# A hybrid gMLP / RG-LRU layer in FP32 on one core: a merge-gate tile joins each turn of the recurrent loop, merge gates wait in DRAM, and the loop's GpSimd work moves to VectorE and ScalarE

## The chip, the cores and the metric

The kernel runs on one core of a Trainium2 chip. Its engines are TensorE (PE in the rows, its weight loads PEld), VectorE (DVE), ScalarE (ACT), GpSimd (POOL) and SyncE (SP), which here only issues DMAs. Each engine carries out its own instructions strictly in program order and waits, at the head of its list, for whatever an instruction needs from another engine. The metric is the device time of one launch in microseconds.

## The reference

The kernel computes one layer of a diffusion backbone for 128 context tokens and 1024 latent tokens (1152 in all) of width 1024, all in FP32:

```python
h = rmsnorm(x, g_pre_mix) * (1 + sc1) + sh1
u, v, xr, gr, ga, gb = split(h @ w_in)             # six blocks of 1024 columns
y_g = sgu(gelu(u), gelu(v), ...)                   # spatial gating in chunks of 128 tokens
xc = depthwise_conv(xr, width 4)
r, ig = sigmoid(block_diag(xc) + b)                # per direction, 16 heads of 64 channels
a = exp(-8 * r * softplus(-lam)); bx = sqrt(1 - a*a) * ig * xc
h_rnn = scan_forward(a, bx) + scan_backward(a, bx) # h[t] = a[t] h[t-1] + bx[t]
y_r = h_rnn * gelu(gr)
merged = sigmoid(ga) * (y_g @ w_br_g) + sigmoid(gb) * (y_r @ w_br_r)
x = x + g1 * rmsnorm(merged @ w_out)
x = x + g2 * rmsnorm(relu(h2 @ w_ff1)**2 @ w_ff2)
```

The six modulation vectors (sh1, sc1, g1, sh2, sc2, g2) are products of a conditioning vector with `w_ada`; the last four are built on VectorE in the middle of the kernel.

## The kernel before

**Column tiles.** Channels lie on the partitions and tokens along the row. Most of the work is a series of "column tiles": 128 output channels for all 1152 tokens, in three chunks of 384 tokens, contracted over 8 blocks of 128 channels. To keep FP32 accuracy each operand is split into a high and a low part, and a product is three passes (high x high, high x low of the data, low of the weights x high), so a tile is 8 x 3 x 3 = 72 matmuls of 128x384. A tile named `xr`, `gr`, `ga`, `gb`, `u` takes its columns from `w_in`; `br` and `bg` are the two branch projections.

**Weights.** The list `stream` (lines 88 to 97) holds the tiles in the order in which TensorE takes them. `w_load` fetches a tile's raw weights by a DMA on SP, `w_hi` makes the high part `wh` (a cast, L120 on ScalarE or L122 on GpSimd), `w_lo` the low part `wl` (a subtraction on VectorE, L129), and `w_convert` does both. `w_next`, at the start of a tile, converts what is not yet converted and issues the loads of the next two.

**Banks.** A tile fills one of two groups of three PSUM banks (`P3`), in turn; the group is free again when its eviction has read it.

**The recurrent loop** (lines 564 to 625, nine turns). Turn j computes the tiles `xr(j+1)` and `gr(j+1)`, and between their matmuls, after the 12th and 30th of xr and the 30th and 54th of gr, the four gate steps `g` (L442, six matmuls each), each followed by two tanh on ScalarE (L448). Beside that, VectorE does the convolution of the next tile (L421, L425), the decay (L478, L479), the input terms, two scans (L498) and the low parts. GpSimd does the high parts of the next two weight tiles (L122), the gate weights' cast (L400), and `finish` (L499): the sum of the two scans and its product with the GELU gate (L504, L506), whose result it stores to DRAM (`d_yr`, L508). The GELU of gr(j+1) is taken at the start of the next turn. The last two turns run gb0 to gb3 in place of xr and gr, and gb4 follows.

**The merge gates.** gb0 to gb4 are held in SBUF as `tb`. The loop over the `br` tiles multiplies each by its gate (L705) and stores it to DRAM (`d_mr`); gb5 to gb7 stand between br0 to br3, and after each of these eleven tiles VectorE takes one step of the later modulations (`ada_steps`: four passes over two blocks of `w_ada`, L675 or L677); a finished modulation is summed over partitions by an all-reduce on GpSimd (L660). Then come ga0 and ga1 with eight loads of v weights (`wv_load`, four after each), the v matmuls (`pv`), ga2 to ga7, the u tiles and the bg tiles, which read the `ta` gates from SBUF.

All temporaries share one pool of 48 SBUF slots.

Of the kernel before, what the change touches and what calls it, by code (L numbers as in the profile page):

```python
# [8 lines left out]
F32 = mybir.dt.float32  # L9
# [5 lines left out]
P = 128  # L15
# [10 lines left out]
# columns of the packed per-channel vectors, each block [channel % 128, channel // 128]  # L26
# [6 lines left out]
def tile_layer(ctx: ExitStack, tc: tile.TileContext, x, vec, rows, bsp, w_spT, ident_in, w_ada1, w_ada, w_in, w_gate,  # L33
# [28 lines left out]
    d_yr = [tc.dram_tile([P, NT], F32, name=f"d_yr{j}") for j in range(KT - 1)]  # L62
    d_x1 = [tc.dram_tile([P, D], F32, name=f"d_xa{t}") for t in range(NTT)]
    d_mod = [[tc.dram_tile([1, D], F32, name=f"d_mod{m}{v}") for v in range(2)] for m in range(4)]

    # ---------------------------------------------------------------- constants
# [7 lines left out]
    # silu of the two conditioning vectors, interleaved [k, (sample, prompt)]  # L74
# [11 lines left out]
    # ---------------------------------------------------------------- weights, one 128-column tile at a time  # L86
    w_in_cols = {"u": 0, "xr": 16, "gr": 24, "ga": 32, "gb": 40}
    stream = []
    for j in range(KT):
        stream += [("xr", j), ("gr", j)]  # L90
    stream += [("gb", 0), ("gb", 1), ("gb", 2), ("gb", 3), ("gb", 4)]
    for j in range(KT):
        stream += [("br", j)] + ([("gb", j + 5)] if j + 5 < KT else [])
    stream += [("ga", j) for j in range(KT)]
# [40 lines left out]
    def w_next(kind, j, ahead=True, load=True):  # L135
        """the split tile of this position; the next one is split meanwhile, the one after it loaded"""
# [17 lines left out]
    def colmm(ps, W, X, cs=range(NC3), ks=range(KT), between=None, at=()):  # L154
        """ps[:, c, :CW] = (W_hi + W_lo).T @ (X_hi + X_lo), without lo * lo; a step of `between` at some points"""
# [11 lines left out]
    # ---------------------------------------------------------------- first norm, first modulation (sh1, sc1)  # L167
# [4 lines left out]
    # the two vectors, hi in columns 0 and 1 and lo in columns 2 and 3 of a full stationary tile  # L172
# [50 lines left out]
    # softplus(-lam) = max(-lam, 0) + log1p(exp(-|lam|)); log1p(e) = 2 atanh(e / (2 + e))  # L223
# [32 lines left out]
    def warm_up(n):  # L256
        """matmuls for their time alone, which keep the tensor engine at its full clock over a wait"""
        for i in range(n):
            pe.matmul(pm1[0], sils[:, 0, :], sils[:, :4, :].rearrange("p k n -> p (k n)"), start=True, stop=True)
# [69 lines left out]
    with tc.tile_pool(name="pa", bufs=2, space=PSUM, reuse_waits="tile") as pa:  # L329
# [34 lines left out]
        def k_both(k):  # L364
            """the passes with X_lo last"""
# [29 lines left out]
        # ------------------------------------------------------------ recurrent branch  # L395
# [168 lines left out]
        for j in range(KT + 1):  # L564
            more = j + 1 < KT
            kx, kg = ((("xr", j + 1), ("gr", j + 1)) if more else (("gb", 2 * (j + 1 - KT)), ("gb", 2 * (j + 1 - KT) + 1)))
            if pgr and j < KT:
                gg[j] = gelu(pgr)
# [601 lines left out]
```

## Time and profile before

| | us |
|---|---|
| three runs: lowest, median, highest | 1852.48, 1853.08, 1853.35 |
| profiled execution, its span | 1852.7 |
| TensorE busy in it | 1798.5 (97%) |
| VectorE, ScalarE, GpSimd busy | 988.3, 621.6, 208.1 |

The profiled execution gives its span alone and no other time; it stands 0.4 us below the median of the runs. Times in the rows are microseconds from the start of the span; `x3` is the number of instructions that a row holds, `[5.06 <-issue]` is the idle time of that engine just before the row and what ended it, where "issue" means that the profile shows no releaser. In the views by stretch, PEclk is the TensorE clock that was granted, 1.00 being 2.4 GHz and 0.50 being 1.2 GHz. Shapes are partitions x elements.

### The profile page before, as it was taken

The page shows a single profiled execution, that of the slowest core. Times are in us where ns is not written, and L with a number is a line of the kernel's source. Part 1 is how long each engine was busy: PE and PEld are TensorE (multiplying, and loading weights), DVE is VectorE, ACT ScalarE, POOL GpSimd, SP SyncE. Part 2 cuts the span into 40 slices and gives each one's busy share as a digit, 9 for nine tenths or more (in the row PEclk, how much of TensorE's full clock was granted, in tenths as well). Part 3 has the DMA queues.
Part 4 walks back from the last instruction along what each step waited for, and adds up shares of the span by engine and source line. Part 5 has one row for each costly group of instructions (what it writes and reads, how often), then busy time and mean ns, then how long its engine had stood idle before and what let it go on. Part 6 is the DMA issues. An engine that isn't in the chain of part 4 may idle for free.

```text
span 1852.7 us, 22285 instructions
## 1 busy us (share of the span) xinstructions
PE 1798.5 (97%) x9504; PEld 1679.8 (91%) x9504; DVE 988.3 (53%) x1013; ACT 621.6 (34%) x857; POOL 208.1 (11%) x159
## 2 busy tenths in 40 slices
PE   7899889899999999999999999999999999999998
PEld 5799889799998899999988899999999999999996
DVE  6859999985662163225453432444444444444447
ACT  7378766731112221223246643111111111111112
POOL 4203343311320031000001100000000000000001
PEclk9999999899999999999999999999999999999999
DMA  8101111243471031103252401111111111011134
GB/s 333 46 29 46 55 53 55 88 157 133 155 248 41 12 114 46 35 23 121 84 160 91 164 30 46 46 35 46 46 44 37 46 46 38 32 46 46 46 137 159
DMA packets 47506, 148.84 MB, mean 80 GB/s; under 512 B 8984, under 2 KB 9256, under 8 KB 47408
## 3 DMA queue, kind: packets, MB, share of 16 engines
q1 hardware_dynamic: 46400, 143.31, 22.6%
q0 software_dynamic: 1008, 4.13, 0.6%
q8 instruction: 74, 1.21, 0.3%
q14 instruction: 24, 0.20, 0.0%
HBM read 129.09 MB, written 18.33 MB: 80 GB/s over the span
## 4 chain that ended last, share of the span: by engine, by line
PE 78%; DVE 2%; DMA 0%; POOL 0%; issue 0%; DVEq 0%; POOLq 0%; ACT 0%; ACTq 0%
PE pf L152 21%; PE p L1090 7%; PE p L1091 7%; PE p L1089 7%; PE u L152 5%; PE br L152 5%; PE ga L152 5%; PE bg L152 5%; PE gb L152 2%; PE po L934 2%; PE po L935 2%; PE po L933 2%; PE pv L748 2%; PE pv L746 2%; PE pv L747 2%; PE s L784 1%
## 5 line engine op out<-in xcount | busy, mean ns | idle before, releaser
L1074 DVE TENSOR_TENSOR acc<-p,acc 128x512 f32<-128x512 f32 x252 | 169.2, 689 | 113.3 <-PE p L1091 113.2
L1090 PE MATMUL p<-w2l,fh 128*128 128x512 f32 x576 | 224.7, 390 | 0.4 <-DVE w2l L1008 0.4
L1091 PE MATMUL p<-w2h,fl 128*128 128x512 f32 x576 | 224.7, 390 | 0.0
L1089 PE MATMUL p<-w2h,fh 128*128 128x512 f32 x576 | 224.3, 389 | 0.0
L120 ACT ACTIVATE wh<-wr 128x1024 fp32r<-128x1024 f32 x70 | 73.4, 1053 | 330.2 <-PE p L1090 236.8
L152 PE MATMUL pf<-h2l,wh 128*128 128x384 f32 x768 | 178.6, 335 | 0.0
L152 PE MATMUL pf<-h2h,wh 128*128 128x384 f32 x768 | 178.5, 335 | 0.0
L152 PE MATMUL pf<-h2h,wl 128*128 128x384 f32 x768 | 178.2, 334 | 0.0
L1000 DVE TENSOR_TENSOR f<-f 128x1152 f32<-128x1152 f32 x32 | 43.5, 1358 | 252.2 <-ACT f L999 252.2
L152 PEld LDWEIGHTS pf<-h2h,wh 128*128 128x128 f32 x768 | 137.3, 188 | 1.1
L999 ACT ACTIVATE f<-pf 128x384 f32<-128x384 f32 x96 | 40.4, 492 | 291.1 <-PE pf L152 291.1
L152 PEld LDWEIGHTS pf<-h2l,wh 128*128 128x128 f32 x768 | 137.4, 188 | 0.0
L152 PEld LDWEIGHTS pf<-h2h,wl 128*128 128x128 f32 x768 | 137.2, 188 | 0.0
L1090 PEld LDWEIGHTS p<-w2l,fh 128*128 128x128 f32 x576 | 108.2, 188 | 22.9 <-DVE w2l L1008 0.8
L1091 PEld LDWEIGHTS p<-w2h,fl 128*128 128x128 f32 x576 | 108.2, 188 | 22.5
L1089 PEld LDWEIGHTS p<-w2h,fh 128*128 128x128 f32 x576 | 108.2, 188 | 22.1
L129 DVE TENSOR_TENSOR wl<-wr,wh 128x1024 fp32r<-128x1024 f32 x86 | 105.3, 1228 | 40.5 <-ACT wh L120 38.3
L448 ACT ACTIVATE th<-g,hbg 64x1152 f32<-64x1152 f32 x64 | 77.9, 1217 | 49.1 <-PE g L442 40.5
L83 POOL TENSOR_SCALAR ssf<-ssf 128x1 f32<-128x1 f32 x9 | 1.7, 191 | 778.4 <-ACT jk L1021 778.3
L660 POOL PARTITION_ALL_REDUCE adr<-ada x8 | 55.8, 6981 | 241.1 <-PE pv L748 102.7
L677 DVE SCALAR_TENSOR_TENSOR ada<-wa,sil,ada 128x1024 f32<-128x1024 f32 x56 | 72.6, 1356 | 3.0 <-DMA wa<-in_w_ada 3.0
L55 DVE TENSOR_TENSOR fl<-f,fh 128x1152 fp32r<-128x1152 f32 x32 | 43.5, 1358 | 39.5 <-ACT fh L54 39.5
(215 smaller groups left out, 3533.0 us busy)
## 6 DMA issues: line engine op xcount, KB each, us to landing
wa<-in_w_ada SPq DMA_DIRECT2D x48, 512.0 KB, 6.6
wr<-in_w_in SPq DMA_DIRECT2D x40, 512.0 KB, 3.5
wr<-in_w_ff SPq DMA_DIRECT2D x32, 512.0 KB, 3.8
w2r<-in_w_ff SPq DMA_DIRECT2D x32, 512.0 KB, 3.5
x<-in_x SPq DMA_DIRECT2D x9, 512.0 KB, 6.7
d_mr<-mr SPq DMA_DIRECT2D x8, 576.0 KB, 3.2
mrl<-d_mr SPq DMA_DIRECT2D x8, 576.0 KB, 3.8
xe<-in_x SPq DMA_DIRECT2D x9, 512.0 KB, 4.8
```

The lines of the kernel that those rows point to most:

```text
L55: (eng or dve).tensor_tensor(lo, src, f32(hi), op=ALU.subtract)
L120: act.activation(hi, raw, AF.Copy)
L129: (eng or dve).tensor_tensor(lo, wopen.pop(i), f32(hi), op=ALU.subtract)
L152: pe.matmul(ps(c), w[:, k * P:(k + 1) * P], X[k][v](c), start=k == 0 and p == 0, stop=k == KT - 1 and p == 2)
L448: act.activation(chunks(th[2 * d + (g ^ h)][o, :]), ps[q, :, :CW], AF.Tanh, scale=0.5, bias=hbg[q, col:col + 1])
L660: pool.partition_all_reduce(o, t, P, ReduceOp.add)
L677: dve.scalar_tensor_tensor(a[v], raw, sc, a[v], op0=ALU.mult, op1=ALU.add)
L1000: dve.tensor_tensor(f, f, f, op=ALU.mult)
L1074: dve.tensor_tensor(a[:, s], ps[t, h], a[:, s], op=ALU.add)
L1089: pe.matmul(ps, fh, wh, start=start, stop=False)
L1090: pe.matmul(ps, fh, wl, start=False, stop=False)
L1091: pe.matmul(ps, fl, wh, start=False, stop=stop)
```

## The change

Turn j of the loop now runs three column tiles, `xr(j+1)`, `gr(j+1)` and `gb(j)`; turn 7 runs gb7 and ga0, turn 8 ga1 and ga2, and ga3 follows the loop. Then stand all eight br tiles in a row, ga4, the eight v-weight loads, the v matmuls, and ga5 to ga7. All sixteen merge gates go to DRAM after their tanh (`d_tb`, `d_ta`, 576 KB each) and are read again one tile ahead of their use (`tbl`, `tal`). In the loop the casts `w_hi` are ScalarE's, `finish` is VectorE's and its store SP's; GpSimd keeps the gate weights' cast (now L401), one copy of two state columns and the all-reduces. The GELU of gr(j+1) stands right behind its tile. The modulation steps take one place per br tile and a second one after br0, br2, br4 and br6; one follows ga4, three lie in the second half of the v matmuls and three beside ga5 to ga7.

```diff
     d_yr = [tc.dram_tile([P, NT], F32, name=f"d_yr{j}") for j in range(KT - 1)]
+    d_ta = [tc.dram_tile([P, NT], F32, name=f"d_ta{j}") for j in range(KT)]
+    d_tb = [tc.dram_tile([P, NT], F32, name=f"d_tb{j}") for j in range(KT)]
...
     for j in range(KT):
-        stream += [("xr", j), ("gr", j)]
-    stream += [("gb", 0), ("gb", 1), ("gb", 2), ("gb", 3), ("gb", 4)]
-    for j in range(KT):
-        stream += [("br", j)] + ([("gb", j + 5)] if j + 5 < KT else [])
-    stream += [("ga", j) for j in range(KT)]
+        stream += [("xr", j), ("gr", j)] + ([("gb", j - 1)] if j else [])
+    stream += [("gb", KT - 1)] + [("ga", j) for j in range(4)]
+    stream += [("br", j) for j in range(KT)]
+    stream += [("ga", j) for j in range(4, KT)]
...
-        def finish(j, th, eng):
+        def finish(j, th):
             h = th[1]
-            eng.tensor_tensor(h, h, th[3], op=ALU.add)
+            dve.tensor_tensor(h, h, th[3], op=ALU.add)
             y = U("yr")
-            eng.tensor_tensor(y, h, gg.pop(j), op=ALU.mult)
+            dve.tensor_tensor(y, h, gg.pop(j), op=ALU.mult)
             if j + 1 < KT:
-                pool.dma_start(d_yr[j], y)
+                sp.dma_start(d_yr[j], y)
...
-        def gb_tanh(ps):
-            t = U("tb")
+        def gate_tanh(ps, name):
+            t = U(name)
             act.activation(chunks(t), ps[:, :, :CW], AF.Tanh, scale=0.5)
             return t
+        def gb_tanh(j, ps):
+            sp.dma_start(d_tb[j], gate_tanh(ps, "tb"))
+        def ga_tanh(j, ps):
+            sp.dma_start(d_ta[j], gate_tanh(ps, "ta"))
...
         pool.memset(warm, 0.0)
-        gg, xcs, tb = {}, {}, {}
+        gg, xcs = {}, {}
...
             more = j + 1 < KT
-            kx, kg = ((("xr", j + 1), ("gr", j + 1)) if more else (("gb", 2 * (j + 1 - KT)), ("gb", 2 * (j + 1 - KT) + 1)))
-            if pgr and j < KT:
-                gg[j] = gelu(pgr)
+            kx, kg = (("xr", j + 1), ("gr", j + 1)) if more else (("gb", j), ("ga", 0)) if j < KT else (("ga", 1), ("ga", 2))
...
                 xcn = conv(j + 1, xr)
+                del xr
                 nxt = xcn, [U("xs", F32R), U("xs", F32R)]
             else:
-                tb[kx[1]] = gb_tanh(px)
+                if j < KT:
+                    gb_tanh(j, px)
+                else:
+                    ga_tanh(1, px)
...
             pgr = col_matmul(*kg, between=steps, at=(30, 54))
-            i = wpos[0]
-            w_hi(i, pool)
-            w_lo(i)
-            w_hi(i + 1, pool)
             if more:
-                raw, gw = gate_hi(j + 1)
+                gg[j + 1] = gelu(pgr)
+                w_convert(wpos[0])
+            else:
+                ga_tanh(kg[1], pgr)
+            del pgr
...
                 del tpp
-            w_lo(i + 1)
+            if more:
+                raw, gw = gate_hi(j + 1)
+                pgb = col_matmul("gb", j)
+                gb_tanh(j, pgb)
+                del pgb
+            i = wpos[0]
+            w_hi(i)
+            w_lo(i)
+            w_hi(i + 1)
...
                 head_lo(*nxt)
+            w_lo(i + 1)
             if prev:
                 scan(j - 1, 1, xcp, thp, ms[1])
-                late = j - 1, thp, pool if j < KT else dve
+                late = j - 1, thp
                 del xcp, thp, ms
             if j == KT - 1:
                 yr_load(range(3))
-                tb[1] = gb_tanh(pgr)
...
         yr_load(range(3, KT - 1))
-        tb[3] = gb_tanh(pgr)
         finish(*late)
-        del xc, prev, pgr, xr, gw, xcn, steps, late, tps
+        del xc, prev, gw, xcn, steps, late, tps
         yr_split(range(3, KT - 1))
-        tb[4] = gb_tanh(col_matmul("gb", 4))
+        ga_tanh(3, col_matmul("ga", 3))
...
         Y = [(acc(h), acc(l)) for h, l in yrs]
+        tbl = {}
+        def tb_load(j):
+            if j < KT:
+                tbl[j] = U("tbl")
+                sp.dma_start(tbl[j], d_tb[j])
+        def ada_step():
+            ada_row()
+            next(ada, None)
+        tb_load(0)
         for j in range(KT):
             W = w_next("br", j)
+            tb_load(j + 1)
             ps = P3("br")
             colmm(pc(ps), W, Y)
             mr = U("mr")
-            dve.scalar_tensor_tensor(chunks(mr), chunks(tb.pop(j)), 1.0, ps[:, :, :CW], op0=ALU.add, op1=ALU.mult)
+            dve.scalar_tensor_tensor(chunks(mr), chunks(tbl.pop(j)), 1.0, ps[:, :, :CW], op0=ALU.add, op1=ALU.mult)
             sp.dma_start(d_mr[j], mr)
-            ada_row()
-            next(ada)
-            if j + 5 < KT:
-                tb[j + 5] = gb_tanh(col_matmul("gb", j + 5, ahead=True))
-                ada_row()
-                next(ada)
+            ada_step()
+            if j % 2 == 0:
+                ada_step()
         del Y, yrs, mr
-        tha = []
...
             colmm(pc(ps), W, X)
-            t = U("ta")
-            act.activation(chunks(t), ps[:, :, :CW], AF.Tanh, scale=0.5)
-            tha.append(t)
+            ga_tanh(j, ps)
-        ga_matmul(0)
-        ada_row()
-        next(ada)
-        for k in range(4):
+        ga_matmul(4)
+        for k in range(KT):
             wv_load(0, k)
-        ga_matmul(1)
-        for k in range(4, KT):
-            wv_load(0, k)
-        ada_row()
-        next(ada)
+        ada_step()
...
                     wv_load(1, t)
+                if h == 1 and t in (1, 4, 7):
+                    ada_step()
...
                     act.activation(vt[h * 4 + g][:, t, :], ps[:, g * P:(g + 1) * P], AF.Gelu_apprx_tanh)
+            for k in range(KT):
+                del wv[h, k]
...
                 dve.reduce_sum(ssv[:, g, :], jk, axis=mybir.AxisListType.X)
-        wv.clear()
...
         sp.dma_start(bspt, bsp.to_broadcast([P, KT * P]).rearrange("p (g q) -> p g q", g=KT))
-        for j in range(2, KT):
+        for j in range(5, KT):
             ga_matmul(j)
-            ada_row()
-            next(ada, None)
-            if j == 2:
+            ada_step()
+            if j == 5:
                 dve.reduce_sum(ssum, ssv.rearrange("p g t -> p t g"), axis=mybir.AxisListType.X)
                 rsqrt_mean(rv[:, :NTT], ssum, 1e-6)
-            for g in ((0, 1, 2) if j == 2 else (j,)):
+            for g in range(3 * (j - 5), min(3 * (j - 4), KT)):
...
         mg = [None] * 3
-        mrl = {0: None}
+        mrl, tal = {}, {}
...
             sp.dma_start(mrl[j], d_mr[j])
+            tal[j] = U("tal")
+            sp.dma_start(tal[j], d_ta[j])
...
             colmm(pc(ps), W, Y)
-            t = tha[j]
-            tha[j] = None
+            t = tal.pop(j)
```

Three places show how the instructions move; a name's number is that of its buffer.

On ScalarE, around the end of a gr tile in a turn of the loop, before (`th` are the gates' tanh, `xs` the high part of the convolved tile, `gg` the GELU of gr):

```order
L448 ACTIVATE th_2144<-g_2179,hbg 64x1152
L448 ACTIVATE th_2143<-g_2179,hbg 64x1152
L457 ACTIVATE xs_2104<-xc_2095 64x1152
L514 ACTIVATE gg_2242<-gr_2112 128x1152
L448 ACTIVATE th_2259<-g_2261,hbg 64x1152
L448 ACTIVATE th_2260<-g_2261,hbg 64x1152
L448 ACTIVATE th_2260<-g_2288,hbg 64x1152
L448 ACTIVATE th_2259<-g_2288,hbg 64x1152
```

and in the changed kernel (`wh` are high parts of weights, `tb` a merge gate's tanh):

```order
L449 ACTIVATE th_2570<-g_2605,hbg 64x1152
L449 ACTIVATE th_2569<-g_2605,hbg 64x1152
L458 ACTIVATE xs_2530<-xc_2521 64x1152
L515 ACTIVATE gg_2633<-gr_2538 128x1152
L121 ACTIVATE wh_2635<-wr_2418 128x1024
L520 ACTIVATE tb_2732<-gb_2659 128x1152
L121 ACTIVATE wh_2735<-wr_2536 128x1024
L121 ACTIVATE wh_2739<-wr_2657 128x1024
L449 ACTIVATE th_2767<-g_2769,hbg 64x1152
L449 ACTIVATE th_2768<-g_2769,hbg 64x1152
L449 ACTIVATE th_2768<-g_2796,hbg 64x1152
L449 ACTIVATE th_2767<-g_2796,hbg 64x1152
```

The GELU was followed by the next turn's tanh; now the cast of gb's weights stands behind the GELU, and behind gb's tanh the casts for the next xr and gr.

On VectorE, from the low part of the weights of one br tile (`wl`) to that of the next: behind br2, before:

```order
L129 TENSOR_TENSOR wl_3440<-wr_3348,wh_3439 128x1024
L705 SCALAR_TENSOR_TENSOR mr_3516<-tb_2848,br_3443 128x1152
L675 TENSOR_SCALAR ada_3521<-wa_3433,sil 128x1024
L675 TENSOR_SCALAR ada_3522<-wa_3433,sil 128x1024
L677 SCALAR_TENSOR_TENSOR ada_3521<-wa_3435,sil,ada_3521 128x1024
L677 SCALAR_TENSOR_TENSOR ada_3522<-wa_3435,sil,ada_3522 128x1024
L129 TENSOR_TENSOR wl_3534<-wr_3437,wh_3533 128x1024
```

and behind br4 in the changed kernel:

```order
L130 TENSOR_TENSOR wl_4070<-wr_3972,wh_4069 128x1024
L735 SCALAR_TENSOR_TENSOR mr_4148<-tbl_3978,br_4075 128x1152
L694 SCALAR_TENSOR_TENSOR ada_3962<-wa_4063,sil,ada_3962 128x1024
L694 SCALAR_TENSOR_TENSOR ada_3963<-wa_4063,sil,ada_3963 128x1024
L694 SCALAR_TENSOR_TENSOR ada_3962<-wa_4065,sil,ada_3962 128x1024
L694 SCALAR_TENSOR_TENSOR ada_3963<-wa_4065,sil,ada_3963 128x1024
L694 SCALAR_TENSOR_TENSOR ada_3962<-wa_4156,sil,ada_3962 128x1024
L694 SCALAR_TENSOR_TENSOR ada_3963<-wa_4156,sil,ada_3963 128x1024
L694 SCALAR_TENSOR_TENSOR ada_3962<-wa_4158,sil,ada_3962 128x1024
L694 SCALAR_TENSOR_TENSOR ada_3963<-wa_4158,sil,ada_3963 128x1024
L130 TENSOR_TENSOR wl_4171<-wr_4067,wh_4170 128x1024
```

Between two low parts stood one step of the modulations (four rows of `ada`); after a br tile with an even number now stand two.

On SP, around the first loads of v weights (`wvr`), before:

```order
L645 DMA wa_4078<-in_w_ada 128x1024
L645 DMA wa_4080<-in_w_ada 128x1024
L110 DMA wr_4082<-in_w_in 128x1024
L645 DMA wa_4167<-in_w_ada 128x1024
L645 DMA wa_4169<-in_w_ada 128x1024
L693 DMA wvr_4171<-in_w_in 128x512
L693 DMA wvr_4176<-in_w_in 128x512
```

and in the changed kernel:

```order
L736 DMA d_mr_72<-mr_4447 128x1152
L662 DMA wa_4454<-in_w_ada 128x1024
L662 DMA wa_4456<-in_w_ada 128x1024
L111 DMA wr_4458<-in_w_in 128x1024
L528 DMA d_ta_84<-ta_4537 128x1152
L710 DMA wvr_4540<-in_w_in 128x512
L710 DMA wvr_4545<-in_w_in 128x512
```

The loads of v weights stood right behind loads; now the store of ga4's gate (`d_ta`) stands ahead of them in the same queue.

## Rows read from the trace of the kernel before

**Rows 1.** The page: the span, and busy time by engine (share, instructions).

```profile
span 1852.7 us, 22285 instructions
...
PE 1798.5 (97%) x9504; PEld 1679.8 (91%) x9504; DVE 988.3 (53%) x1013; ACT 621.6 (34%) x857; POOL 208.1 (11%) x159
```

**Rows 2.** Waits of TensorE by line and releaser: total us, times, longest.

```profile
PE xr L152 <- issue: 13.3, 3, 5.1
...
PE g L442 <- ACT th L448: 9.2, 2, 9.0
...
PE gb L152 <- issue: 3.5, 1, 3.5
```

**Rows 3.** Timeline of TensorE: start, length, instruction [idle before].

```profile
49.77 0.50 PE L203 MATMUL pm<-wal,sils 128*128 128x512 f32 x1 [1.24 <-DVE wal L55]
...
83.21 0.68 PE L152 MATMUL xr<-hh,wh 128*128 128x384 f32 x3
83.73 0.68 PE L152 MATMUL xr<-hl,wh 128*128 128x384 f32 x3
...
204.03 0.66 PE L152 MATMUL xr<-hh,wh 128*128 128x384 f32 x1 [5.06 <-issue]
...
239.77 0.88 PE L152 MATMUL xr<-hh,wh 128*128 128x384 f32 x3 [3.60 <-issue]
...
394.98 0.77 PE L152 MATMUL br<-yrh,wh 128*128 128x384 f32 x3
```

**Rows 4.** By stretch: busy us of PE, PEld, DVE, ACT, POOL; granted clock, DMA share, GB/s.

```profile
46.00:52.00 6.00, 4.34 (x18) 3.21 (x18) 6.00 (x3) 4.66 (x6) 6.00 (x3) 1.00 0.09 11
...
204.00:209.00 5.00, 4.97 (x16) 5.00 (x17) 5.00 (x2) 2.12 (x2) 4.62 (x3) 0.50 0.36 108
...
83.20:395.00 311.80, 284.68 (x1563) 280.62 (x1562) 284.65 (x233) 218.62 (x189) 98.75 (x59) 0.95 0.17 58
```

**Rows 5.** Timeline of three engines at the end of a gb tile.

```profile
445.02 0.68 PE L152 MATMUL br<-yrh,wh 128*128 128x384 f32 x3
445.22 1.14 ACT L519 ACTIVATE tb<-gb 128x1152 f32<-128x1152 f32 x1 [10.03 <-PE gb L152]
...
446.25 1.05 ACT L120 ACTIVATE wh<-wr 128x1024 fp32r<-128x1024 f32 x1
...
447.33 1.23 DVE L129 TENSOR_TENSOR wl<-wr,wh 128x1024 fp32r<-128x1024 f32 x1 [2.16 <-ACT wh L120]
```

**Rows 6.** Timeline of VectorE and GpSimd while `finish` runs beside the decay.

```profile
203.12 3.07 DVE L479 TENSOR_SCALAR th<-th 128x1152 f32<-128x1152 f32 x1
...
209.94 0.76 DVE L479 TENSOR_SCALAR th<-th 128x1152 f32<-128x1152 f32 x1
...
201.85 3.73 POOL L504 TENSOR_TENSOR th<-th,th 128x1152 f32<-128x1152 f32 x1
```

**Rows 7.** Timeline of ScalarE: a gate step's two tanh, and two casts of `yr`.

```profile
214.12 2.45 ACT L448 ACTIVATE th<-g,hbg 64x1152 f32<-64x1152 f32 x2 [1.63 <-PE g L442]
...
385.55 2.29 ACT L54 ACTIVATE yrh<-yrl 128x1152 fp32r<-128x1152 f32 x2 [0.94 <-DVE th L498]
```

**Rows 8.** Timeline of VectorE and GpSimd in the br tiles: modulation steps and an all-reduce.

```profile
464.99 9.15 DVE L677 SCALAR_TENSOR_TENSOR ada<-wa,sil,ada 128x1024 f32<-128x1024 f32 x4 [0.18 <-DMA wa<-in_w_ada]
...
482.66 1.36 DVE L705 SCALAR_TENSOR_TENSOR mr<-tb,br 128x1152 f32<-128x1152 f32 x1 [5.67 <-PE br L152]
483.93 4.87 DVE L677 SCALAR_TENSOR_TENSOR ada<-wa,sil,ada 128x1024 f32<-128x1024 f32 x4
...
467.64 7.00 POOL L660 PARTITION_ALL_REDUCE adr<-ada  x1 [12.81 <-DVE ada L677]
```

**Rows 9.** DMA issues: queue, count, KB each, median us to landing.

```profile
wvr<-in_w_in SPq DMA_DIRECT2D x16, 256.0 KB, 2.6
...
yrl<-d_yr SPq DMA_DIRECT2D x7, 576.0 KB, 5.7
```

**Rows 10.** Timeline of SP: four issues of v-weight loads.

```profile
537.60 3.32 SPq L693 DMA_DIRECT2D wvr<-in_w_in  x4
```

## The prediction, made before the changed kernel ran

> **What bounds the kernel now.** The page first: TensorE is busy 1798.5 of 1852.7 us [rows 1], so time can only be lost or won where it stands still or is clocked down. The view of waits says where. Three lines matter, six waits together: 13.3 + 9.2 + 3.5 = 26.0 us [rows 2], and the lines named (xr, g, gb) are all of the recurrent loop and its tail. The timeline of TensorE bounds that stretch: from the first xr at 83.21 to the first br matmul at 394.98 [rows 3], 311.8 us. How much of it is work? Three matmuls take 0.52 us (83.21 to 83.73, [rows 3]), one 0.1733, a column tile of 72 takes 12.48. The stretch holds seven turns of 144 matmuls, eight times 24 for the gate steps and five gb tiles: 1008 + 192 + 360 = 1560, or 270.4 us. It loses 41.4. 26.0 are the waits; the rest is the clock. Over the stretch the granted clock is 0.95, and 0.05 of 311.8 is 15.6; in the 5 us behind the wait of 5.06 it was 0.50 [rows 4], that is 1.2 GHz, which loses 2.5. Six such falls lose 15, so each of the six waits cost 2.5 more than its length. A shorter wait did not do that: around the wait of 1.24 [rows 3] the clock stayed at 1.00 [rows 4].
>
> Who holds TensorE in the loop? VectorE is busy 284.65 of the 311.8 us [rows 4]; a turn lasts 35.74 (204.03 to 239.77, [rows 3]) where its 168 matmuls take 29.1. Part of VectorE's load is GpSimd's doing: the same tensor_scalar takes 3.07 us beside GpSimd's addition and 0.76 without it [rows 6].
>
> **The change, part by part.** Matmuls are neither added nor removed. Seven tiles, gb0 to gb6, go into the turns, gb7 and ga0 to ga3 into the tail; I compare what the loop loses, before and after.
>
> *VectorE and GpSimd in the loop.* `finish` adds 2 x 1.36 us to VectorE (an operation of that shape, [rows 8]), a third tile a low part of 1.23 [rows 5]; the end of contention gives back 2.3 at the row shown and, by my estimate, as much at its neighbour. So VectorE needs about 35 us a turn, of a turn that has 240 matmuls, 41.6 us. It is no longer what TensorE waits for. If that were all, the loop would lose nothing.
>
> *The high parts on ScalarE: the term that decides.* Before, GpSimd cast the next two tiles' weights while TensorE was at work. In the changed order on ScalarE the cast of gb's weights stands behind the GELU of gr, which waits for the last matmul of gr, and the casts for xr behind gb's tanh, which waits for the last matmul of gb. TensorE therefore stands still at the end of the tile for eviction and cast, and the trace has this chain: gb ends at 445.02, its tanh begins 0.20 later, the cast begins 1.03 after that and takes 1.05 [rows 5]. That is 2.28; with a tenth each for the signal to TensorE and its restart I take 2.5. It occurs 16 times: seven times from gr to gb, seven from gb to the next tile, ga0 to ga1 and ga2 to ga3. To this come, per turn, 0.3 at gr to gb (ScalarE reaches the GELU late, behind tanh pairs of 2.45 [rows 7]), twice 0.12 for the low part (1.23 on VectorE [rows 5], against six matmuls, 1.04, that need only the high part), and 0.25 as an allowance for a gate step that finds ScalarE with a cast. A turn loses 2.5 + 2.5 + 0.3 + 0.25 + 0.25 = 5.8 and lasts 47.4; seven turns lose 40.6.
>
> *The clock at these waits.* 2.5 us lies between the wait of 1.24, which left the clock at 1.00, and the shortest that was followed by a fall, 3.5 [rows 2 to 4]. I take no fall, since 1.2 us lie between it and one, 1.0 between it and the other, and TensorE works a full tile ahead of each; the other value is a rival below.
>
> *The tail.* The two hand-overs there cost 5.0. The first three `yr` loads now stand on SP behind the store of ga0's gate. After ga0's end: 1.23 for the tanh [rows 5], four issues, some 1.3, and 5.7 to land [rows 9], so 8.2; the last of three casts of 1.15 ends at 9.4, and the tanh pair of 2.45 queued behind these casts [rows 7] is done at 12.0. TensorE wants that bank in ga1 at 2.5 + 36 x 0.1733 = 8.7 and waits 3.3. `finish` stands on the same queue with its own store and may add up to 3; I take 5.0, with the clock 7.5 (0.8, if the loads land in half the time, to 9.7).
>
> The loop then loses 40.6 + 5.0 + 7.5 = 53.1 against 41.4: **+11.7** (+5 to +14).
>
> *Two modulation steps behind a br tile.* One step takes 4.87, mr 1.36 [rows 8], the low part 1.23: 7.5 us of VectorE in a tile of 12.48, no wait, and none stands in the waits of before. Two steps make 12.33, plus 0.2 for the tile's end: 12.5, which is level with the tile. But a step beside an all-reduce takes 9.15 [rows 8], 4.3 more. By the order of steps such a one falls behind br2 (its second step; the low part of br4 comes some 4 late) and behind br6 (the low part of ga4, some 3); with 0.2 and 0.5 elsewhere **+8**. Below: 0, if loads of `w_ada` space the steps out so that the all-reduce lies beside a single step; above: 13, with two clock falls of 2.5.
>
> *The v weights.* Before, half of the loads stood behind loads on SP. Now all eight stand behind the store of ga4's gate, which waits for its tanh: 1.23, one issue of some 0.4 for the store, one of 0.83 (a quarter of 3.32, [rows 10]), 2.6 to land [rows 9], then cast and low part, at half the width at most 1.05 and 1.23 and by my estimate 0.6 and 0.7. That is 6.4 of standstill after ga4, some 0.4 less because the first matmuls need only the high part; with a clock fall of 2.5 **+8.5** (5.5 if there is no fall, 11 if later loads, 0.83 apart, fall behind too).
>
> *At nothing.* 32 transfers of 576 KB to and from DRAM: the DMA engines are at 0.17 in the loop [rows 4], and a reload is issued a tile of 12.48 ahead and lands in 5.7 [rows 9]; uncovered, the first would cost that 5.7. The wait for `pst` goes. The three late modulation steps beside v and the normalisation beside ga5 to ga7 are work that VectorE had there before.
>
> The sum: 11.7 + 8 + 8.5 = 28.2; 1852.7 + 28.2 = 1880.9, **1881 us**. The profiled execution gives only its span, 0.4 below the median of the runs, 1853.08, and I leave that out. Its own bounds: 1852.7 + 5 + 0 + 5.5 = 1863 and 1852.7 + 14 + 13 + 11 = 1891.
>
> **The rivals.**
>
> *The clock falls at the short hand-overs.* Each of 16 would lose 2.5 more: 40, and 1921; if it happens at every second one, 1901. For it: no wait of 2.5 us stands in the trace, and each of the six longer ones in the loop was followed by a fall. Against it: the 1.24 us without one. The Trainium skill, TensorE: Matmul & The Clock Gate, section A second HAM failure mode: psum-queue depth-cycling, says that a kernel whose TensorE idles briefly between groups of matmuls, as it moves from bank to bank, had its clock swing to and fro; by that rule this case would come about. The trace so far shows falls after long waits alone.
>
> *VectorE stays the bound.* If the gate weights' cast, which GpSimd keeps, and slower evictions hold VectorE, its chain (eviction, convolution, decay, scan) has little to spare before the low part of xr, by my walk 0.3 us. With 2 us more each of six turns loses 2: 12, and 1893, with clock falls some 1905. Against it: GpSimd's additions, the cause of the row of 3.07, are gone [rows 6].
>
> *The casts are not late: faster.* If ScalarE had each high part ready when a tile ends, the 16 hand-overs would cost nothing but a restart; the loop would lose some 53.1 - 40 = 13, that is 28 less than before, and with + 16.5 behind it the time would be 1841. The point from which this decides is a hand-over of 0.7 us: 2.5 - 28.2 / 16. Against it stands the order on ScalarE, in which the cast follows an instruction that reads the tile's end, and whose tanh alone takes 1.03 [rows 5].
>
> *The loop moves, but nothing changes.* The waits of before go (41.4) and the new ones cost as much, with the br tiles and v weights hidden: 1853.
>
> **How the numbers follow.** A measurement of this kernel can tell some 0.2%, 3.7 us, from no change. The forecast has 0.60, the clock 0.27, VectorE 0.05, the faster case 0.05, no change 0.03. The range takes the forecast's bounds, 1863 to 1891, and reaches to 1904, to take in VectorE and the half of the clock's case that stays at or below every second hand-over; above it are left some 0.13, below some 0.08. Faster 0.05, the same 0.03, slower 0.92.
>
> **What the profile will show.** Right: the waits of TensorE name the cast of `wh` on ScalarE at gb and xr, some 14 times about 2.4 us, and a turn of 47 us; VectorE idles several us in each turn; one wait of over 5 us at the first pv matmul for `wv`; waits for `wl` at br4 and ga4. The step on the clock is right if the clock is 1.00 behind the hand-overs, wrong if it falls there. Wrong would be hand-overs under 1 us, or a turn over 50 us with VectorE full.

## The result and the profile of the changed kernel

The changed kernel takes 1902.1 us (median of four runs, 1900.5 to 1903.1) against 1852.8 for the kernel before: a ratio of 1.0264 with a 95% interval of 1.0250 to 1.0278, 49 us slower. The forecast was 1881 with a range of 1863 to 1904: the sign was right, the time is inside the range, and the loss is 1.75 times the 28.2 us that were forecast. Of the forecast's own bounds, 1863 and 1891, the time is 11 above the upper one. The profiled execution took 1901.8 with a span of 1899.8; a span is some 2 us shorter than the time of the same execution, so the 1852.7 to which the forecast adds its sum, a span too, answers to the 1899.8: 47.1 more, where the medians differ by 49.3.

The page of the changed kernel, which answers to [rows 1]:

```profile
span 1899.8 us, 22349 instructions
...
PE 1821.3 (96%) x9504; PEld 1695.0 (89%) x9504; DVE 968.3 (51%) x1027; ACT 640.1 (34%) x875; POOL 118.0 (6%) x120
```

Its view of waits of TensorE (line and releaser: total us, times, longest), which answers to [rows 2]:

```profile
PE gb L153 <- ACT wh L121: 21.1, 8, 2.7
PE xr L153 <- ACT wh L121: 13.0, 6, 2.2
...
PE pv L766 <- ACT wv L712: 6.1, 1, 6.1
PE ga L153 <- ACT wh L121: 4.5, 2, 2.3
PE g L443 <- ACT th L449: 4.4, 1, 4.4
...
PE br L153 <- DVE wl L130: 3.0, 1, 3.0
```

The waits of before are gone, and 16 waits for a cast of `wh` stand in their place, 38.6 us together. TensorE's matmuls are the same 9504, yet its busy time rose by 22.8 us: the same work, for the most part at a lower clock (the mean granted clock of the span is 0.981 where it was 0.989, which makes some 16 of them). Its timeline shows where (start, length, instruction, idle before), the answer to [rows 3]:

```profile
81.72 0.68 PE L153 MATMUL xr<-hh,wh 128*128 128x384 f32 x3
...
111.63 0.79 PE L153 MATMUL gb<-hh,wh 128*128 128x384 f32 x3 [2.71 <-ACT wh L121]
128.15 0.79 PE L153 MATMUL xr<-hh,wh 128*128 128x384 f32 x3 [2.16 <-ACT wh L121]
...
179.01 0.79 PE L153 MATMUL xr<-hh,wh 128*128 128x384 f32 x3 [2.16 <-ACT wh L121]
...
475.56 2.29 PE L443 MATMUL g<-xs,gw 128*128 128x384 f32 x6 [4.42 <-ACT th L449]
...
515.53 0.77 PE L153 MATMUL br<-yrh,wh 128*128 128x384 f32 x3
...
569.73 1.26 PE L153 MATMUL br<-yrh,wl 128*128 128x384 f32 x3 [2.97 <-DVE wl L130]
...
639.23 0.80 PE L766 MATMUL pv<-wv,hh 128*128 128x512 f32 x1 [6.11 <-ACT wv L712]
```

Here a turn, from xr to xr, lasts 50.86 us (128.15 to 179.01); its two hand-overs, the idle of TensorE from the end of one tile to the start of the next, are 2.71 and 2.16 in every turn, within 0.01. The loop with its tail runs from 81.72 to 515.53, 433.8 us; its 26 tiles and 192 gate matmuls need 357.7, so it loses 76.1 where the kernel before lost 41.4. By stretches (busy us of TensorE, its granted clock, DMA share, GB/s), the answer to [rows 4]:

```profile
81.72:515.53 433.81, 390.80 (x2067) 0.94 0.19 66
...
112.00:115.00 3.00, 3.00 (x13) 0.57 0.02 5
...
128.15:179.01 50.86, 45.99 (x241) 0.93 0.14 48
229.50:234.50 5.00, 4.67 (x25) 1.00 0.67 227
229.83:278.95 49.12, 44.25 (x241) 0.97 0.18 62
515.53:639.23 123.70, 114.62 (x651) 0.98 0.68 241
639.23:645.20 5.97, 5.97 (x14) 0.52 1.01 365
```

Behind the hand-over at 111.63 the clock is 0.57 for 3 us, and it fell behind twelve of the fourteen hand-overs of the turns. Two, at 229.83 and 380.25, were not followed by a fall; the turn that begins with the first of them is 49.12 long in place of 50.82 and 50.86 (the turns ahead of it), so a fall costs 1.7 us. Over the loop, 0.06 of 433.8 is 26 us of clock beside 43.0 us of waits (38.6 and the gate step's 4.4); some 7 of the 76.1 are left that neither names.

The chain that was forecast from [rows 5], in the timeline of ScalarE and VectorE ahead of the xr at 128.15:

```profile
126.02 1.13 ACT L520 ACTIVATE tb<-gb 128x1152 f32<-128x1152 f32 x1 [14.44 <-PE gb L153]
127.05 2.00 ACT L121 ACTIVATE wh<-wr 128x1024 fp32r<-128x1024 f32 x2
...
128.13 1.22 DVE L130 TENSOR_TENSOR wl<-wr,wh 128x1024 fp32r<-128x1024 f32 x1 [15.29 <-ACT wh L121]
```

The tanh waits for gb's last matmul, the cast starts 1.03 later, and VectorE has stood idle for 15.29 us when it comes. That is the longest of its idles: from 179.01 on it has more to do, and is busy 32.65 us of a turn of 50.82 (179.01 to 229.83), where before it was busy 35.21 of 35.74 (204.03 to 239.77).

The three longer waits, each with the instructions that made it. For the gate step, SP, then ScalarE:

```profile
461.77 0.33 SPq L528 DMA_DIRECT2D d_ta<-ta  x1
462.19 0.38 SPq L509 DMA_DIRECT2D d_yr<-yr  x1
462.68 2.65 SPq L538 DMA_DIRECT2D yrl<-d_yr  x3
...
469.06 1.17 ACT L54 ACTIVATE yrh<-yrl 128x1152 fp32r<-128x1152 f32 x1 [5.28 <-DMA yrl<-d_yr]
...
473.06 2.44 ACT L449 ACTIVATE th<-g,hbg 64x1152 f32<-64x1152 f32 x2
```

For br4, VectorE and GpSimd (to compare with [rows 8]):

```profile
560.36 5.80 DVE L692 TENSOR_SCALAR ada<-wa,sil 128x1024 f32<-128x1024 f32 x2 [0.94 <-DMA wa<-in_w_ada]
...
568.47 1.21 DVE L130 TENSOR_TENSOR wl<-wr,wh 128x1024 fp32r<-128x1024 f32 x1
...
558.52 7.10 POOL L677 PARTITION_ALL_REDUCE adr<-ada  x1 [46.57 <-DVE ada L694]
```

For v, SP and ScalarE (to compare with [rows 10]):

```profile
634.32 0.33 SPq L528 DMA_DIRECT2D d_ta<-ta  x1
634.69 4.32 SPq L710 DMA_DIRECT2D wvr<-in_w_in  x8
...
638.54 1.28 ACT L712 ACTIVATE wv<-wvr 128x512 fp32r<-128x512 f32 x2 [4.26 <-DMA wvr<-in_w_in]
```

In the first and the third piece the loads stand behind the gate's store, where the forecast put them. In the second, two modulation steps make the low part of br4 late: two passes beside the all-reduce take 5.80, the two behind it 2.46, and 0.94 is a wait for a load of `w_ada`.

The sum over stretches: the time ahead of the loop is 1.5 shorter (81.72 against 83.21), the loop loses 34.7 more, the br tiles and ga4 up to v lose 11.4 (123.7 for nine tiles of 12.48) where the same stretch before lost nothing, and the rest is some 2.6 longer, since v starts at a clock of 0.52. That is 47.1, the difference of the spans.

### The profile page after: what moved, and what is told of

It is laid out like the page before. It is cut to its first block, busy times and chain, and to the rows that moved or that the text cites. A ratio compares the mean times of both kernels' runs of the same rounds, so it can differ in the third digit from the quotient of the medians.

```text
span 1899.8 us, 22349 instructions
## 1 busy us (share of the span) xinstructions
PE 1821.3 (96%) x9504; PEld 1695.0 (89%) x9504; DVE 968.3 (51%) x1027; ACT 640.1 (34%) x875; POOL 118.0 (6%) x120
## 4 chain that ended last, share of the span: by engine, by line
PE 86%; ACT 2%; DMA 1%; issue 1%; DVE 1%; SPq 0%; DVEq 0%; POOLq 0%; POOL 0%; ACTq 0%
PE pf L153 21%; PE p L1111 7%; PE p L1112 7%; PE p L1110 7%; PE u L153 5%; PE bg L153 5%; PE ga L153 5%; PE br L153 5%; PE gb L153 5%; PE xr L153 4%; PE gr L153 2%; PE pv L767 2%; PE pv L766 2%; PE pv L768 2%; PE po L954 2%; PE po L955 2%
## 5 line engine op out<-in xcount | busy, mean ns | idle before, releaser
L121 ACT ACTIVATE wh<-wr 128x1024 fp32r<-128x1024 f32 x88 | 91.4, 1052 | 333.4 <-PE p L1111 236.8
L153 PE MATMUL gb<-hh,wh 128*128 128x384 f32 x192 | 49.0, 366 | 21.1 <-ACT wh L121 21.1
```

Of the source, the lines that this page charges most:

```text
L121: act.activation(hi, raw, AF.Copy)
L153: pe.matmul(ps(c), w[:, k * P:(k + 1) * P], X[k][v](c), start=k == 0 and p == 0, stop=k == KT - 1 and p == 2)
```

## The experiments

Theory: the 16 hand-overs cost twice, by their wait and by the clock behind them; the cast stands behind an instruction that reads the end of a tile. Rivals: the third tile fills some engine or queue, and the wait only names the cast; the clock falls for another reason; it is ScalarE's speed and not the place; or the longer waits in the tail come from busy DMA engines. All comparisons are with runs of the kernel before on the same chip, 1852.8 to 1853.3.

**Casts a tile earlier.**

```diff
-            pgr = col_matmul(*kg, between=steps, at=(30, 54))
+            pgr = col_matmul(*kg, between=steps, at=(30, 54), ahead=True)
...
-                pgb = col_matmul("gb", j)
+                pgb = col_matmul("gb", j, ahead=True)
```

> In the changed kernel the casts of the weights' high parts are moved a tile ahead: those of gb and of the two ga tiles stand on ScalarE at the start of gr (ga0, ga2), those of xr at the start of gb; nothing else changes. Theory (each hand-over costs its wait, 38.6 us in 16, and a clock fall of some 1.7 us behind 14 of them): a turn falls from 50.8 to about 42.5 us, the clock in the turns is 1.00, and the time is 1902 - 38.6 - 24 + some 4 for what is late next in the tail = 1835 to 1850. Rival (the third tile fills VectorE, ScalarE or the DMA queues, and the wait only names the cast): a turn stays above 47 us and the time above 1885.

Measured: 1854.0 us, ratio to before 1.0009 (1.0000 to 1.0019). All 16 hand-overs are gone from the view of waits, and a turn is 42.77 long with the clock at 1.00. The stretch of one turn (TensorE's busy us, clock, DMA share, GB/s):

```profile
146.90:189.67 42.77, 41.90 (x241) 1.00 0.12 39
```

The two longest waits that this run has and the changed kernel has not, or has shorter:

```profile
PE g L443 <- ACT th L449: 15.3, 8, 9.2
...
PE pst L652 <- POOL states L501: 6.6, 1, 6.6
```

The timeline of ScalarE around the start of a gr tile:

```profile
143.46 1.04 ACT L121 ACTIVATE wh<-wr 128x1024 fp32r<-128x1024 f32 x1
144.41 2.43 ACT L449 ACTIVATE th<-g,hbg 64x1152 f32<-64x1152 f32 x2
```

48 us came back by two words, so the third tile does not fill the turn. The time is 4 over the expected range because TensorE, now earlier, meets other waits: 0.9 in each turn for a tanh that the early cast holds up, 9.2 in the tail for the tanh behind the yr casts, 6.6 for the scan states.

**Only gr's end.** The first of the two edits above alone.

> Only the casts at gr's end are moved a tile ahead (gb's in seven turns, ga1's and ga3's); the hand-over from gb to the next xr stays. Theory: nine hand-overs go (seven of 2.7, two of 2.2 to 2.3 us, 23.4 in all) with some nine clock falls of 1.7: 1902 - 23 - 15 = 1864, between 1858 and 1870; the other seven keep 2.2 us and their falls. Rival (what fills the turn lies elsewhere): less than 15 us gained, since the wait reappears at the next xr.

Measured: 1881.8 us, ratio 1.0157 (1.0141 to 1.0172), a gain of 20 where 32 to 44 were expected. The rival's bound was 15. The 2.30 at gb to xr stayed, as expected, and was followed by a fall in four of six turns (some 47.1 long in place of 45.6; what sets the two others apart stays open). The miss is in the tail: the same 9.1 at the gate step and 7.5 for the states, and 0.9 a turn, as in the run before. These come to some 18 us (9.1 less 4.4, 7.5 and seven times 0.9), and 1881.8 less 18 is the 1864 that was expected: the gain of a hand-over was right, what is late next was left out.

**Matmuls that fill the hand-over.** 14 matmuls behind each gr and 11 behind each gb, whose result is not read.

```diff
+        def fill(n):
+            t = P1("fill")
+            for i in range(n):
+                pe.matmul(t[:, :CW], X[0][0](0)[:, :P], X[0][0](0), start=True, stop=True)
...
+                fill(14)
                 pgb = col_matmul("gb", j)
                 gb_tanh(j, pgb)
+                fill(11)
```

> The changed kernel, with matmuls for their time alone put into the hand-overs of the seven turns: 14 of 128x384 (2.4 us) behind each gr, 11 (1.9 us) behind each gb; their result is not read. TensorE then waits under 0.5 us. Theory (the falls come from TensorE standing still for over 2 us): the clock in the turns stays at 1.00, the hand-overs are as long as before, and 12 falls of 1.7 us go: 1902 - 20 = 1882, between 1876 and 1886. Rival (the clock falls for another reason, such as the load of three tiles a turn): 1900 or more, clock still 0.93 in a turn.

Measured: 1885.0 us, ratio 1.0174 (1.0159 to 1.0189), inside the range. The timeline of TensorE at one hand-over:

```profile
108.47 2.59 PE L562 MATMUL fill<-hh 128*128 128x384 f32 x14
111.35 0.79 PE L153 MATMUL gb<-hh,wh 128*128 128x384 f32 x3 [0.29 <-ACT wh L121]
```

The stretch of one turn (busy us of TensorE, clock, DMA share, GB/s):

```profile
126.49:174.19 47.70, 47.15 (x265) 1.00 0.16 52
```

The hand-overs are as long as before, the clock stays at 1.00 and a turn takes 47.70: the forecast of a turn was 47.4 under the assumption of no fall. The clock in the turns is worth 17 us by itself.

**The tail alone.** yr loads ahead of the store of ga0's gate, v loads ahead of ga4's, one modulation step per br tile.

```diff
+                if j == KT - 1:
+                    yr_load(range(3))
                 ga_tanh(kg[1], pgr)
...
             ada_step()
-            if j % 2 == 0:
-                ada_step()
...
+            if j == 4:
+                for k in range(KT):
+                    wv_dma(0, k)
+                for k in range(4):
+                    wv_load(0, k)
             ga_tanh(j, ps)
```

> The loop's turns stay; three edits behind them. The first yr loads stand on SP ahead of the store of ga0's gate; the loads of v weights ahead of the store of ga4's gate and half their casts ahead of its tanh; one modulation step behind each br tile, the others beside v. Theory (queue order and VectorE's load make these three waits): the gate step's wait of 4.4 falls to about 1, the wait at br4 of 3.0 goes, that for v of 6.1 falls to about 1, and with each a clock fall of 2 to 3 us: 1902 - 18 = 1884, between 1879 and 1889. Rival (the loads are late because the DMA engines are busy, 0.68 in the br tiles, not because of their place in the queue): the wait for v stays above 4 us and the time above 1892.

Measured: 1886.9 us, ratio 1.0182 (1.0165 to 1.0199), a gain of 15, inside the range. The waits at the gate step and at br4 are gone; for v the view of waits still has

```profile
PE pv L778 <- DVE wv L721: 4.2, 2, 4.0
```

v now starts with its tile, and the low parts come late: VectorE takes 9.32 us for eight of them beside two all-reduces on GpSimd, as the timelines of both show, where five took 3.37 in the changed kernel.

```profile
620.99 9.32 DVE L721 TENSOR_TENSOR wv<-wvr,wv 128x512 fp32r<-128x512 f32 x8 [4.86 <-ACT wv L720]
...
613.99 14.34 POOL L678 PARTITION_ALL_REDUCE adr<-ada  x2 [30.40 <-DVE ada L695]
```

The theory of the queues holds for the gate step, and the load of VectorE for br4. For v the wait stays at the 4 that the rival named, but its row names VectorE's low part and no DMA.

**The casts on GpSimd again, nothing else.**

```diff
-                w_convert(wpos[0])
+                w_hi(wpos[0], pool)
+                w_lo(wpos[0])
...
-            w_hi(i)
+            w_hi(i, pool)
             w_lo(i)
-            w_hi(i + 1)
+            w_hi(i + 1, pool)
```

> The changed kernel with the loop's casts of high parts on GpSimd again, at the same places in the program; the third tile, the gates in DRAM and finish on VectorE stay. GpSimd's list has no instruction ahead of the cast that reads the tile's end. Theory (it is the place behind the tile's eviction that costs, not the engine's speed): the 16 hand-overs go as in the run with early casts, and ScalarE is free of the 0.9 a turn: 1843 to 1856. Rival (GpSimd's casts slow VectorE beside them, and the third tile makes that tell): a turn above 45 us, 1870 or more.

Measured: 1842.1 us, ratio 0.9939 (0.9925 to 0.9954): faster than the kernel before, and 60 us faster than the change. The casts stand at the same lines of the program; GpSimd's list there holds nothing that reads the end of a tile. A turn has next to nothing left to give (busy us of PE, PEld, DVE, ACT, POOL; clock, DMA share, GB/s):

```profile
150.69:192.51 41.82, 41.82 (x241) 41.55 (x241) 30.65 (x27) 26.73 (x24) 3.88 (x6) 1.00 0.15 51
```

41.82 us for 240 matmuls, which need 41.6, TensorE busy throughout, VectorE 30.65. In the turns behind it VectorE is busy 33.4, where the run with early casts has 32.65: where its casts run beside VectorE, GpSimd slows it no more than the third tile can cover. The margin is small. In GpSimd's list the casts for xr stand behind a copy of two state columns (L501), which waits for VectorE's scan; in one of these turns they end at 246.12, 0.7 us ahead of the xr that needs them (246.82).

**`finish` on GpSimd again, nothing else.**

```diff
-            dve.tensor_tensor(h, h, th[3], op=ALU.add)
+            eng = pool if j < KT - 1 else dve
+            eng.tensor_tensor(h, h, th[3], op=ALU.add)
...
-                sp.dma_start(d_yr[j], y)
+                pool.dma_start(d_yr[j], y)
```

> The changed kernel with finish (sum of the scans, product with the GELU gate, store) on GpSimd again for tiles 0 to 6. Theory (VectorE is off the path in the loop of three tiles): no difference, 1902 within 4, a turn 50 to 51 us. Rival (VectorE's chain reaches the low part of xr with nothing to spare): GpSimd slows it again, and the time is above 1908.

Measured: 1902.0 us (two runs), ratio 1.0263 (1.0242 to 1.0283). No difference: VectorE was off the path in the changed loop.

**Parts of the move in the old loop.** First the casts on ScalarE together with `finish` on VectorE, two tiles a turn and the gates in SBUF.

```diff
-            w_hi(i, pool)
+            w_hi(i)
             w_lo(i)
-            w_hi(i + 1, pool)
+            w_hi(i + 1)
...
-            eng.tensor_tensor(h, h, th[3], op=ALU.add)
+            dve.tensor_tensor(h, h, th[3], op=ALU.add)
...
-                pool.dma_start(d_yr[j], y)
+                sp.dma_start(d_yr[j], y)
```

> The kernel before with one part of the change alone: the casts of the loop on ScalarE at their old places (ahead of the GELU), finish on VectorE, its store on SP; two tiles a turn, gates in SBUF as before. Theory (VectorE set the turn of 35.75 us, some 5 of them by GpSimd's contention, against 2.7 for finish): a turn falls to 32 to 33.5, the waits for xr with their clock falls shrink, and the time is 1825 to 1842. Rival (ScalarE's casts stand in the chain eviction, convolution, split and lengthen it by as much): within 6 of 1853.

Measured: 1881.8 us, ratio 1.0154 (1.0139 to 1.0169), against both theories. The view of waits:

```profile
PE xr L152 <- ACT wh L120: 25.8, 6, 6.8
```

The timeline of ScalarE ahead of one of these waits:

```profile
208.19 1.16 ACT L457 ACTIVATE xs<-xc 64x1152 fp32r<-64x1152 f32 x1 [5.47 <-DVE xc L425]
...
212.88 2.00 ACT L120 ACTIVATE wh<-wr 128x1024 fp32r<-128x1024 f32 x2
```

Here the cast stands behind `xs`, which waits for VectorE's convolution. It is the same mechanism with another instruction ahead of the cast. Then `finish` alone on VectorE, the casts left with GpSimd (the last two pieces of that diff):

> The kernel before with finish on VectorE and its store on SP; the casts stay GpSimd's, two tiles a turn. Theory (VectorE sets the turn, and GpSimd's additions slow it by 4.7 us against 2.7 that finish adds): a turn of 35.75 falls by some 2 us, and the time to about 1840, between 1834 and 1847. Rival (contention and the added work cancel): within 4 of 1853.

Measured: 1840.2 us, ratio 0.9931 (0.9916 to 0.9946), as expected. A turn of the old loop falls from 35.75 to 33.72, with VectorE still nearly full. Here a wait of 4.72, ahead of 202.20, with a fall behind it, and one of 1.30, ahead of 235.92, with none, stand side by side in two turns (columns as above):

```profile
202.20:235.92 33.72, 32.42 (x168) 31.85 (x169) 33.08 (x29) 25.60 (x23) 6.30 (x5) 0.91 0.18 58
235.92:269.63 33.71, 29.73 (x168) 28.98 (x169) 33.07 (x29) 25.61 (x23) 6.30 (x5) 1.00 0.17 57
```

**All repairs together.** First with ScalarE's casts, gb's moved on into the gap behind gr's, and the yr tiles split in turns 6 and 7.

> All repairs together: every cast of a tile's weights one or two tiles ahead (gb's in ScalarE's gap behind the cast for gr), the yr loads and splits spread over turns 6 and 7, one modulation step behind each br tile, the loads and casts of v weights at the start of ga4, and the transpose of the scan states behind br1. Theory: the hand-overs, the gate step's 0.9 a turn and 9.2 in the tail, the 6.6 for the states, br4 and the first v matmul all go, a turn comes to 41.8 to 42.3 us, and the time is 1854 less 15 + 6.6 + 6.1 + 3 and some 8 of clock = 1815 to 1828. Rival (something not in the list of waits, such as VectorE's chain at the end of the loop, takes their place): above 1835.

Measured: 1840.2 us, ratio 0.9928 (0.9912 to 0.9945): the rival's side. A turn is 41.8, but the gate steps in the tail wait 6.3 and 8.6. The timeline of ScalarE ahead of the first of them:

```profile
384.35 1.22 ACT L449 ACTIVATE th<-g,hbg 64x1152 f32<-64x1152 f32 x1 [3.97 <-DVE th L499]
```

A tanh that needs only TensorE's result waits for a scan of another tile. The early splits hold two of the 48 buffers each, and the tanh takes one that the scan gives back; that this is the reason is argued from the row (ahead of the second wait the same idle is 7.13), and no run with more buffers was made. Then with the yr loads early, their splits late, and the casts on GpSimd or on ScalarE:

```diff
+                if j == KT:
+                    for k in range(3):
+                        hi, lo = U("yrh", F32R), U("yrl", F32R)
+                        act.activation(hi, yr[k], AF.Copy)
+                        yrs.append((hi, lo))
                 ga_tanh(kg[1], pgr)
...
+            if j == KT:
+                for k in range(3):
+                    dve.tensor_tensor(yrs[k][1], yr.pop(k), f32(yrs[k][0]), op=ALU.subtract)
...
             W = w_next("ga", j)
+            if j == 4:
+                for k in range(KT):
+                    wv_load(0, k)
```

> The run with the loop's casts on GpSimd, and behind the loop's turns: the first yr loads ahead of the store of ga0's gate, their casts beside ga2 and their low parts behind the first scan, one modulation step behind each br tile, the loads and casts of v weights at the start of ga4, the transpose of the states behind br1. Theory (the waits left there come from these queues): 9.0 at the gate step, 6.3 at v and 4.9 for wl in br and ga go, with three or four clock falls of 2 to 3 us: 1842 - 20 - 8 = 1814, between 1810 and 1824. Rival (as in the run with all repairs, a shortage of buffers or VectorE's chain at the loop's end takes their place): 1828 or more.

Measured: 1827.5 us, ratio 0.9860 (0.9843 to 0.9876), the fastest of all, 26 us below the kernel before and 75 below the change; just over the expected range. What is left in the view of waits:

```profile
PE pv L775 <- ACT v L779: 3.4, 1, 3.4
PE ga L153 <- POOL wh L123: 3.3, 1, 3.3
```

The second of these is the mechanism of the change once more, now on GpSimd, as its timeline ahead of this tile shows:

```profile
428.37 1.17 POOL L501 COPY states<-th 128x1 f32<-128x1 f32 x1 [16.93 <-DVE th L499]
429.47 4.29 POOL L123 CAST wh<-wr 128x1024 fp32r<-128x1024 f32 x2
```

The cast stands behind the copy of the states, which waits for VectorE's last scan, and beside VectorE's low parts of yr two casts take 4.29 us, where two take 2.03 earlier in the same run (at 398.99).

> The same repairs on the version whose early casts are ScalarE's. Theory (a cast that has no instruction ahead of it that reads the tile's end costs nothing on either engine): within 5 us of the run with GpSimd's casts, 1812 to 1826. Rival (ScalarE's casts stand ahead of the gates' tanh and cost there): 8 us or more above it.

Measured: 1831.8 us, ratio 0.9885 (0.9870 to 0.9900), 4.3 above its twin, within the 5 expected but beyond the range: 4.8 and 2.7 us of waits at the first br tiles for low parts on VectorE. The turns are as long as with GpSimd.

## Why the prediction was right, and where its size was off

**Direction and place: right.** The sixteen hand-overs are where the order on ScalarE put them. Forecast were 2.8 for gr to gb and 2.5 for gb to the next tile; measured 2.71 and 2.16. Moving the same cast ahead brings 48 us, putting it on an engine whose list does not read the tile's end brings 60.

**The step that failed** is "I take no fall". The waits of 2.2 to 2.7 us lie between a wait that left the clock alone and those that were followed by a fall. I took no fall for my 2.5, although by the distances that I gave (1.2 to the harmless wait, 1.0 to the shortest harmful one) the other side was the nearer. The clock fell behind twelve of fourteen in the turns, so the forecast's rival on the clock happened at most of the hand-overs, at 1.7 us each where that rival had 2.5. It is luck that the time agrees with the 1901 of that rival's half, and the range holds it only because it was stretched from 1891 to 1904 to take in that half. The Trainium skill, TensorE: Matmul & The Clock Gate, section A second HAM failure mode: psum-queue depth-cycling, describes this swing of the clock at brief idles; the trace agrees, with 0.93 over a turn and 1.00 once the idles are filled. The run that fills them shows the price apart from the waits, 17 us, and a turn of 47.70 at full clock. The loop lost 76.1 where I had 53.1; those 23 us are the miss, and 26 of the 76.1 are clock, of which I had counted only 2.5 behind the gate step's wait. Why two of the fourteen were not followed by a fall stays open.

**A wait misread.** I gave each of six waits of the kernel before a fall of 2.5. One of the two for a gate step is the 0.2 that [rows 2] leave beside the longest of 9.0, and the clock behind it (175.5 to 180.5) stayed at 1.00: five waits had a fall, at some 3 us each. The loss of 41.4 is not touched by it.

**The tail's gate step: right.** 4.4 measured against 5.0, by the queue that was named, and shown by the run in which the loads stand ahead. The size is in part luck: counted from ga0's end the tanh was done after 15 us where I had 12.0, and TensorE came after some 10.6 where I had 8.7, the clock having fallen behind ga0's hand-over.

**Two modulation steps: too high.** The wait at br4 is 3.0 and the only one in that stretch; the one for ga4 did not come. With a clock fall it is some 5 where I had 8.

**The v weights: right.** 6.1 against 6.4 less 0.4, and a slow start of some 3 for the clock where 2.5 was taken.

**Costed at nothing: confirmed** for the DRAM gates in the turns (a turn of 41.82 with all stores in it) and for `finish` on VectorE (no difference when undone). The share of DMA in the br tiles rose to 0.68 (0.52 before, 394.98 to 557), and no wait of TensorE names a `tbl` or `tal` reload.

**The rivals.** VectorE as the bound: a turn is over 50 us, but VectorE is not full in it, as the sign of this rival asked; it is excluded by VectorE's idle of some 18 us a turn and by the run with `finish` undone. The faster case, with casts that are ready in time, did not come about, but its figure of 1841 was close to what the run with GpSimd's casts then measured, 1842.1.

The parts, from the runs: in the old loop `finish` on VectorE brings 13 us, and the casts on ScalarE cost 42 beside it. The third tile with the gates in DRAM, added to `finish` on VectorE and GpSimd's casts, is worth nothing as it stands (1840.2 against 1842.1): from the first xr of the turns to the first br tile TensorE loses 14.7 us where it lost 29.2, but 11.9 up to v and some 2.5 at v's start give that back. With the tail, br4 and v repaired it is 1827.5.

## What to carry to other kernels

Work that another engine can do as fast may still not be moved to it before one has read what stands ahead of it in that engine's list: a cast behind an eviction is a cast behind the end of the tile, however short it is. A wait on TensorE is to be priced with the clock that follows it, and a length between one that is known to be harmless and one that is known to hurt is better priced as hurting when it recurs. Whoever repairs a wait should list what comes second: early casts gained 48 us where GpSimd's casts gained 60, since two waits took their turn that the latter do not have, 0.9 in each of seven turns and 6.6 for the scan states.

## What the runs showed of the hardware that was not expected

Idles of 2.2 to 2.7 us, behind some 14 us (gb) or 30 us and more (xr and gr) of work without a longer wait, were followed by a TensorE clock of 1.2 GHz in twelve of fourteen cases, for 1.7 us lost each time, and two of the same length, 2.16 and 2.17, were not; with the same idles filled by matmuls the clock stayed at 2.4 GHz. A cast of 128x1024 takes GpSimd 1.0 us in the run that gives it the casts, as long as ScalarE (1.05 in [rows 5]), and there a turn has VectorE busy 0.7 us longer than with ScalarE's early casts, while GpSimd's additions beside VectorE had made an operation four times as long [rows 6]. The same cast takes 2.1 us where it runs beside VectorE's low parts of yr.
